# The second layer's experts in 64 slots each: plain float32 products on halves of the array's columns, weights unsplit, outputs summed to the tokens in PSUM

## The chip, the cores and the metric

The kernel runs on one core of a Trainium2 chip. The metric is the device time of one execution in microseconds (us); lower is better. The number compared is the median of several runs, three for the kernel before.

## The reference

A backbone of two layers works on 512 tokens of 1024 channels: 256 context tokens and 256 latent ones. Each layer has four token mixers side by side, an output projection, and then a mixture of 16 experts. The last layer's experts work on the 256 latent tokens alone, since only these are returned. A router chooses for each token the best of four groups of four experts and the two best experts in it. What an expert computes, in float32:

```python
def _moe(h, router_w, router_b, w_gate, w_up, w_down):
    scores = jax.nn.sigmoid(h.astype(F32) @ router_w.astype(F32))
    sel = scores + router_b.astype(F32)
    grp_score = lax.top_k(sel.reshape(-1, N_GROUPS, EXPERTS_PER_GROUP), TOP_K)[0].sum(-1)
    best = jnp.argmax(grp_score, axis=-1)
    in_grp = (jnp.arange(N_EXPERTS) // EXPERTS_PER_GROUP)[None, :] == best[:, None]
    _, idx = lax.top_k(jnp.where(in_grp, sel, -jnp.inf), TOP_K)
    w = jnp.take_along_axis(scores, idx, axis=-1)
    w = w / jnp.sum(w, axis=-1, keepdims=True)
    combine = jnp.sum(jax.nn.one_hot(idx, N_EXPERTS, dtype=F32) * w[..., None], axis=1)
    out = jnp.zeros(h.shape, F32)
    for e in range(N_EXPERTS):
        act = jax.nn.silu(h @ w_gate[e]) * (h @ w_up[e])
        out = out + combine[:, e:e + 1] * (act @ w_down[e])
    return out.astype(h.dtype)
```

Every expert has three matrices, 1024 x 512 (gate), 1024 x 512 (up) and 512 x 1024 (down): 6 MB, and 96 MB for the 16 experts of a layer. Each token needs two experts only, so a kernel can hand each expert just its own tokens. By the reference's routing the fullest expert of the second layer gets 61 of the 256 tokens.

## The kernel before, in words

Tokens are kept transposed (channels on the 128 partitions, tokens along the free axis, `xT`), in eight blocks of 128 channels. The program is written in the order of the model; a scheduler then puts the instructions of each engine into an order, by classes that the code sets with `k.order` and by the order of the code within a class. The change sits in the last stage of the second layer, `moe` (L1696), after which only the final norm and the output follow.

An expert's tokens. `route` (L1600) ranks each token within its two experts. `moe` turns the 256 latent tokens into rows and splits them in two parts, `h2_hi` and `h2_lo`, so that passes in the rounded format F32R carry float32 values exactly. `gather` (L1750) takes two experts at a time: a selection matrix `sel` of zeros and ones is multiplied with the rows (L1762, 32 passes, for each of eight blocks two parts by two tiles of tokens), and the outcome, the tokens of both experts transposed, goes to the tiles `xe` (L1766). An expert has `CAPS[1]` = 96 slots for its tokens. Where an expert had more tokens than slots, a branch (L1801) sends all tokens through every expert; it isn't taken on these inputs.

An expert's weights. They come as six loads of 1 MB, [128, 2048] each (`load`, L1937): two halves of gate (0, 1), two of up (2, 3), two of down (4, 5; these halve the output channels). The ring that they land in has two tracks of three buffers each, and load i goes to track i % 2:

```python
RINGS = (3, 3)
...
lambda e, i: load(I["w_moe"][16 * layer + e, i], which=i % 2)
```

All loads are issued by SP in one fixed order; a load waits there until the last reader of its buffer is done, and the loads behind it wait with it. The first six are asked for ahead of the branch. `parts` (L152, L153) splits each load into a high and a low tile of 1024 columns by two: two ScalarE (ACT) copies and two VectorE (DVE) subtractions per load. After these four the ring buffer is free.

An expert's products. Tokens are the stationary operand (96 columns of the array), weights the moving one, 512 columns at a time. `product` makes three F32R passes for each input block, 24 for gate, 24 for up and 24 for down:

```python
for i, ((xh, xl), (wh, wl)) in enumerate(zip(xs, ws)):
    nc.tensor.matmul(p, xh, wh, start=first and i == 0, stop=False)
    nc.tensor.matmul(p, xh, wl, start=False, stop=False)
    nc.tensor.matmul(p, xl, wh, start=False, stop=last and i == n - 1)
```

Between up and down stand the silu (L1849), the product with up (L1850), four transposes (L1856), and the split of the transposed activations (L1858, L1859). The code issues the next expert's gate product before this expert's down product.

Back to the tokens. The down products are copied out as rows `y` (L1877) and, for the first `VIA` = 15 experts, written to the DRAM tensor `Y` (L1881). Behind the 15th expert, GpSimd (POOL) fetches for each token its two rows from `Y` by indirect DMAs (L1891: `ya`, `yb`), and ACT and DVE weight and add them (L1893, L1894). The last expert's rows come back by a product with a weighted selection matrix, `backT` (L1901); `ya` is added to it in PSUM by products with the identity (L1905). Eight DVE additions put the sum, times the gate of the conditioning, onto `xT` (L1912). Then come the norm's sums of squares (L1319 to L1329), the scaling (L2022) and the output.

PSUM has eight banks: four of track a, two of b, two of p; the pools of 4 KB tiles (`TILES`) hold all that is called `u` in the code.

Of the kernel before, what the change touches and what calls it, by code (L numbers as in the profile page):

```python
# [19 lines left out]
# arguments of a sigmoid are kept above this: exp(-FLOOR) < 2^64, and the sigmoid there is 2e-19  # L20
# [3 lines left out]
def shape_consts():  # L24
    """Constants that depend on shapes alone, one [128, n] block per name."""
# [8 lines left out]
    # diagonal 32x32 blocks: [partition s, column r % 32]  # L34
# [42 lines left out]
# constants that the first steps take; the others follow later  # L77
# [3 lines left out]
class Consts:  # L81
    def __init__(self, nc, pool, src):
        """src: DRAM AP [128, n], the early ones first"""
# [28 lines left out]
class K:  # L112
    """What all parts of the kernel share: engines, pools, constants. Tiles come from the pools of the track (a or b):
    slots of a pool go out in program order, so that what runs side by side takes them from different pools."""
# [41 lines left out]
    def exp_ln(self):  # L156
        """Exp and Ln from one table of ScalarE, from here on"""
# [6 lines left out]
def sigmoid(nc, t):  # L164
    """t = 1 / (1 + t), t holding exp(-x), below 2^64 (what Ln takes)"""
# [11 lines left out]
    # log decays, rows: [token, tile, (dir h dk)], 16 times too large  # L177
# [13 lines left out]
    # cumulative sums within tiles of 128, transposed: [(h dk), token]  # L191
# [8 lines left out]
    # chunk states  # L200
# [30 lines left out]
    # scores within tiles, transposed: [s, h, tile, r]  # L231
# [24 lines left out]
    # two heads at a time, a bank for each  # L256
# [45 lines left out]
    # outputs, transposed  # L302
# [21 lines left out]
def norm_gate(k, oT, gT, center=False):  # L324
    """norm(oT) * silu(gT) in two parts, norms over groups of 64 partitions; all [128, 2, n]; gT is at least FLOOR"""
# [22 lines left out]
def ret(k, qT, kT, v, dlog, t0):  # L348
    """qT: [128 (h%2 dk), 2, tokens from t0*128 on], kT: [128, 2, 512], v: [128, 4, 256] rows,
    dlog: [128, 12] decay logits: (dir h) on all partitions, then (dir hp) by partition."""  # L350
# [9 lines left out]
    # decays  # L360
# [17 lines left out]
    # rotary embedding of the latent tokens  # L378
# [10 lines left out]
    # states  # L389
# [31 lines left out]
    # scores within tiles, transposed  # L421
# [41 lines left out]
def tri_inverse(nc, N, G, X, P):  # L463
    """G = inverse of (I + N), N strictly lower, one 32x32 matrix per partition at [col * 32 + row].
    G holds the identity at first. X: [128, 512] and P: four [128, 1024], scratch."""
# [5 lines left out]
    # pairs  # L471
# [14 lines left out]
    # 16: zero quarters of the triangles are skipped; columns split over the engines  # L486
# [3 lines left out]
    def dot(eng, out, left, right, nr, ncol, nk, scratch):  # L490
        """out[c, r] = sum_k left[k, r] * right[c, k]"""
# [20 lines left out]
def dn(k, dram, xs, cw, gab, prm, t0):  # L512
    """In five steps (a generator), the first four as soon as the projections of k, of the gates, of v and of q are there;
    the last yields the outputs. xs: calls for the q, k, v projections [128 (h%2 d), 2, tokens] (q: from t0*128 on);
    cw: [128, 6, 5] taps, gab: [128, 4, 16] rows (a: dir h | b: dir h), prm: [128, 16] (dt_bias | a_log),
    dram: two scratch tensors [128, 1024] f32."""
# [4 lines left out]
    def conv(n):  # L521
        """Short convolution, silu, unit norm of q and k"""
# [35 lines left out]
    def in_rows(y):  # L558
        """[token, tile, (h d)]"""
# [20 lines left out]
    # log decay and log beta, [token, tile, (dir h)]  # L580
# [14 lines left out]
    # decays from the chunk's start (times beta), to its end: chunks of 32, and of 64 (with the neighbour's sum)  # L595
# [23 lines left out]
    # the same of the later chunk of a pair (from its start) and of the earlier one (to its end): forward the odd ones  # L619
    # are later, backward the even ones  # L620
# [6 lines left out]
    # pair decays [s, dir, tile, h, r] in chunks of 32  # L627
# [19 lines left out]
    def products(y, dec, a):  # L647
        """Products of keys with y, by their decays; tiles from a on"""
# [21 lines left out]
    # inverses, one system (chunk, dir, tile, h) per partition  # L670
# [8 lines left out]
    # the blocks of these systems that link the chunks of a pair: [later token, tile, h, earlier]  # L679
# [38 lines left out]
    # [d][half of the systems] matrices 128 x 128, zeros but for the diagonal 32x32 blocks  # L718
# [15 lines left out]
    # the inverses of pairs of chunks: B, [column, system, row], gets minus later inverse @ link @ earlier inverse  # L734
# [961 lines left out]
def moe(k, I, P, S, h2, xT, mod, load_e, between, layer):  # L1696
# [53 lines left out]
    def gather(e):  # L1750
# [20 lines left out]
        for g in range(2):  # L1771
            if e + g < VIA:
                continue
# [284 lines left out]
```

## Time and profile before

| | |
|---|---|
| device time, median of 3 runs | 1637.6 us (1631.38 to 1642.4) |
| span of the profiled execution, first to last instruction | 1629.0 us |
| TensorE (PE) busy, of that span | 1457.5 us, 11752 instructions |
| VectorE (DVE) | 1164.8 us |
| ScalarE (ACT) | 841.8 us |
| GpSimd (POOL) | 379.7 us |
| mean granted clock of TensorE | 0.936 of full speed |
| bytes moved by DMA | 345.71 MB, mean 212 GB/s |

The profile is one execution on the chip, recorded by the hardware; its engines' busy times are sums over the whole program, in which the stages have different limits. The program has some 1300 us ahead of the second layer's experts, some 310 us of these experts, and some 20 us behind them, so the table alone says little about the stage that changes. The profiled execution's own time is given only as its span; the median of the runs is 8.6 us above it. In the profile's rows, PE stands for matmuls, PEld for the loading of their stationary operand, SPq for SP's queue of DMAs; "128*96 128x512" is a stationary operand of 128 rows and 96 columns with 512 moving columns on 128 partitions. A matmul of F32R is one instruction in the trace; one of plain float32 is two.

### The profile page before, as it was taken

To read this page: it belongs to the slowest core of one execution; us is meant where nothing else is said; L and a number is where in the kernel's file an instruction comes from. 1 tells how busy PE (TensorE), PEld (TensorE's weight loads), DVE (VectorE), ACT (ScalarE), POOL (GpSimd) and SP (SyncE) were. 2 spreads that over 40 slices of the span, in tenths; PEclk is the share of its full clock that TensorE was granted. 3 is DMA by queue.
4 is the path that set the end of the run, shared out by engine and by line. 5 is a ranking of instruction groups with operands and counts; after the bars stand their busy time and mean duration, and the time that the engine had idled before them with its cause. 6 is when DMAs were issued, how large, how long until landed. Compare 5 with 4: busy or idle time off the path is not lost. (4 is left out here: it accounts for less than half of the span.)

```text
span 1629.0 us, 29159 instructions
## 1 busy us (share of the span) xinstructions
PE 1457.5 (89%) x11752; PEld 1159.6 (71%) x11752; DVE 1164.8 (72%) x1696; ACT 841.8 (52%) x1192; POOL 379.7 (23%) x429
## 2 busy tenths in 40 slices
PE   5797879999997999999998788969999799999996
PEld 1686669888665788888886576758867577777774
DVE  6795792667435879787885786874467488888885
ACT  4442214342523758576773533313254488888874
POOL 2745242444210000000004665442242000000001
PEclk9897869999998999999999897969899799999999
DMA  9130352142445878889798221534366199999992
GB/s 387 48 111 27 98 176 103 66 149 100 143 159 203 322 285 348 323 306 363 276 349 320 70 78 57 171 126 140 122 238 239 37 356 351 347 337 362 356 336 103
DMA packets 85991, 345.71 MB, mean 212 GB/s; under 512 B 32582, under 2 KB 37512, under 8 KB 51160
## 3 DMA queue, kind: packets, MB, share of 16 engines
q1 hardware_dynamic: 79784, 320.36, 53.5%
q10 hardware_dynamic: 3840, 13.76, 2.1%
q0 software_dynamic: 2224, 9.63, 1.5%
q8 instruction: 96, 1.57, 0.4%
q14 instruction: 47, 0.39, 0.1%
HBM read 315.05 MB, written 28.67 MB: 211 GB/s over the span
## 5 line engine op out<-in xcount | busy, mean ns | idle before, releaser
L153 DVE TENSOR_TENSOR w_lo<-ring,w_hi 128x1024 fp32r<-128x1024 f32 x384 | 453.8, 1219 | 77.8 <-ACT w_hi L152 75.4
L152 ACT ACTIVATE w_hi<-ring 128x1024 fp32r<-128x1024 f32 x384 | 395.6, 1059 | 91.5 <-PE ps_up L1747 61.5
L1747 PE MATMUL ps_up<-w_lo,xe 128*128 128x512 f32 (+1 forms) x512 | 202.2, 395 | 4.9 <-DVE w_lo L153 4.4
L1746 PE MATMUL ps_up<-w_hi,xe 128*128 128x512 f32 (+1 forms) x512 | 200.5, 394 | 3.2 <-PEq L1801 3.2
L1748 PE MATMUL ps_up<-w_hi,xe 128*128 128x512 f32 (+1 forms) x512 | 200.7, 392 | 0.0
L1380 PE MATMUL ps_project<-h_hi,wi_lo 128*128 128x256 f32 (+1 forms) x568 | 138.9, 311 | 24.7 <-DVE wi_lo L153 24.6
L1380 PE MATMUL ps_project<-h_hi,wi_hi 128*128 128x256 f32 (+1 forms) x568 | 137.6, 310 | 14.3 <-ACT h_hi L1368 8.3
L1380 PE MATMUL ps_project<-h_lo,wi_hi 128*128 128x256 f32 (+1 forms) x568 | 135.0, 303 | 5.4 <-DVE h_lo L1369 5.4
L1380 PEld LDWEIGHTS ps_project<-h_hi,wi_lo 128*128 128x128 f32 (+1 forms) x568 | 99.0, 205 | 33.1 <-DVE wi_lo L153 28.0
L1747 PEld LDWEIGHTS ps_up<-w_lo,xe 128*128 128x128 f32 (+1 forms) x512 | 89.4, 175 | 33.8 <-DVE w_lo L153 9.7
L1380 PEld LDWEIGHTS ps_project<-h_hi,wi_hi 128*128 128x128 f32 (+1 forms) x568 | 98.9, 205 | 19.3 <-ACT h_hi L1368 8.4
L1746 PEld LDWEIGHTS ps_up<-w_hi,xe 128*128 128x128 f32 (+1 forms) x512 | 89.5, 175 | 28.9 <-ACT xe L1766 2.0
L1748 PEld LDWEIGHTS ps_up<-w_hi,xe 128*128 128x128 f32 (+1 forms) x512 | 89.5, 175 | 26.4
L1746 PE MATMUL ps_down<-w_hi,actT 128*128 128x512 f32 (+1 forms) x256 | 100.7, 395 | 5.7 <-ACT actT L1858 5.7
L1380 PEld LDWEIGHTS ps_project<-h_lo,wi_hi 128*128 128x128 f32 (+1 forms) x568 | 98.2, 203 | 8.9 <-DVE h_lo L1369 6.1
L1747 PE MATMUL ps_down<-w_lo,actT 128*128 128x512 f32 (+1 forms) x256 | 100.5, 393 | 1.2 <-DVE w_lo L153 1.2
L1748 PE MATMUL ps_down<-w_hi,actT 128*128 128x512 f32 (+1 forms) x256 | 96.9, 395 | 0.9 <-DVE actT L1859 0.4
L152 ACT ACTIVATE wi_hi<-ring 128x1024 fp32r<-128x1024 f32 (+1 forms) x50 | 51.2, 1032 | 88.1 <-DMA ring<-in_w_in 43.6
L1937 POOL DMA_DIRECT2D ring<-in_w_in x4 | 2.5, 618 | 385.0 <-DMA ring<-in_w_ada 374.8
L153 DVE TENSOR_TENSOR wi_lo<-ring,wi_hi 128x1024 fp32r<-128x1024 f32 (+1 forms) x50 | 69.8, 1401 | 25.3 <-ACT wi_hi L152 19.7
L1766 ACT ACTIVATE xe<-ps_gather 128x384 fp32r<-128x384 f32 (+1 forms) x96 | 48.0, 527 | 65.3 <-PE ps_gather L1762 65.3
L1891 POOL DMA_INDIRECT ya<-Y,rt_slot x6 | 5.8, 965 | 322.7 <-DVE w_lo L153 320.4
(534 smaller groups left out, 3159.7 us busy)
## 6 DMA issues: line engine op xcount, KB each, us to landing
ring<-in_w_moe SPq DMA_DIRECT2D x192, 1024.0 KB
ring<-in_w_ada SPq DMA_DIRECT2D x46, 1024.0 KB
ring<-in_w_in SPq DMA_DIRECT2D x21, 1024.0 KB
ring<-in_w_out SPq DMA_DIRECT2D x8, 1024.0 KB
Y<-y ACTq DMA_DIRECT2D x15, 512.0 KB
Y<-y ACTq DMA_DIRECT2D x15, 384.0 KB
xT<-in_xT SPq DMA_DIRECT2D x8, 512.0 KB
ring<-in_w_in POOLq DMA_DIRECT2D x3, 1024.0 KB
```

The source lines that it names most:

```text
L152: self.nc.scalar.activation(out[0], src, AF.Copy)
L153: self.nc.vector.tensor_tensor(out[1], src, out[0].bitcast(F32), ALU.subtract)
L1380: nc.tensor.matmul(p[:, c], x[a], w[b][:, c], start=i + a + b + o == 0, stop=i == n - 1 and a == 1, skip_group_check=True)
L1746: nc.tensor.matmul(p, xh, wh, start=first and i == 0, stop=False)
L1747: nc.tensor.matmul(p, xh, wl, start=False, stop=False)
L1748: nc.tensor.matmul(p, xl, wh, start=False, stop=last and i == n - 1)
L1766: nc.scalar.activation(x, p, AF.Copy)
L1891: nc.gpsimd.indirect_dma_start(out=o, out_offset=None, in_=Y[:VIA * cap], in_offset=bass.IndirectOffsetOnAxis(ap=slot[:, i, t:t + 1], axis=0))
L1937: queue.dma_start(w[:, :n], src)
```

## The change

The first layer keeps `moe`; two pieces of it become functions of their own, `token_rows` (the rows in two parts) and `overflow` (the branch), with the same code in them. The second layer gets a function of its own, `moe_small`:

- 64 slots per expert and not 96.
- `gather` takes four experts at a time, 256 columns in all, and sums the products of both parts of the rows in PSUM, so that `xe` is one float32 tile and not two parts.
- The weights are not split: the ring's buffers are read by the products themselves, in plain float32. An inward product uses 64 columns of the array; for each input block two matmuls of 256 moving columns, on the left and the right half of the array's columns, take the two halves of gate's (then up's) 512 outputs, which thus lie on the two halves of one PSUM bank's partitions.
- The silu and the product with up work on 128 partitions by 256 columns; two transposes bring the activations back.
- Outward, the two loads (halves of the output channels) go to the two halves of the array's columns, 512 moving columns each.
- Each expert's output is at once multiplied with its weighted selection matrix (`back`), in matmuls that use one half of the array's rows each, and summed over all 16 experts in four PSUM banks (`last`). There are no rows in DRAM and no indirect fetches.

```diff
-CAPS = (128, 96)
+CAPS = (128, 64)
...
+def token_rows(k, h2, nt):
...
+def overflow(k, I, h2, xT, mod, cwo, mxi, nt, cap, layer):
...
+def moe_small(k, I, P, S, h2, xT, mod, load_e, layer):
+    nc, C = k.nc, k.C
+    cap, nt = 64, 2
+    assert CAPS[layer] == cap
+    NT = nt * 128
+    q0 = T - NT
+    k.track = "b"
+    rsel, _, _, cwo, mxi, cw = route(k, h2, P, nt, cap)
+    hi, lo = token_rows(k, h2, nt)
+    def gather(e):
+        sel = k.u("sel", nt * 4 * cap).bitcast(F32R).rearrange("p (t g s) -> p t g s", t=nt, g=4)
+        nc.vector.tensor_tensor(sel, C["row_f"][:, None, None, :cap].to_broadcast([128, nt, 4, cap]),
+                                rsel[:, :, e:e + 4, None].to_broadcast([128, nt, 4, cap]), ALU.is_equal)
+        xs = [k.u("xe", track="b") for _ in range(2)]
+        out = [[] for _ in range(4)]
+        for m in range(0, 8, 2):
+            p = k.bank("gather", "b")
+            for i in range(2):
+                n = 0
+                for rows in (hi, lo):
+                    for t in range(nt):
+                        nc.tensor.matmul(p[:, i * 256:(i + 1) * 256], rows[t][:, (m + i) * 128:(m + i + 1) * 128],
+                                         sel[:, t].rearrange("p g s -> p (g s)"), start=n == 0, stop=n == 2 * nt - 1)
+                        n += 1
+            x = xs[m // 4][:, m % 4 * 256:(m % 4 + 2) * 256]
+            if m % 4:
+                nc.scalar.activation(x, p, AF.Copy)
+            else:
+                nc.vector.tensor_copy(x, p)
+            for i in range(2):
+                for g in range(4):
+                    out[g].append(x[:, i * 256 + g * cap:i * 256 + (g + 1) * cap])
+        return out, sel
+    def back(sel, e):
+        s = k.u("back", nt * 128).rearrange("p (t a s) -> p t a s", t=nt, a=2)
+        nc.vector.tensor_tensor(s, sel[:, :, e % 4].bitcast(F32)[:, :, None].to_broadcast([128, nt, 2, cap]),
+                                cw[:, :, e:e + 1, None].to_broadcast([128, nt, 2, cap]), ALU.mult)
+        p = k.bank("back", "b")
+        for t in range(nt):
+            nc.tensor.transpose(p[:, t * 128:(t + 1) * 128], s[:, t].rearrange("p a s -> p (a s)"), C["ident"])
+        b = k.u("backT", NT)
+        nc.vector.tensor_copy(b, p[:, :NT])
+        return b
+    xs, sel = gather(0)
+    first = [load_e(0, i) for i in range(6)]
+    overflow(k, I, h2, xT, mod, cwo, mxi, nt, cap, layer)
+    ps = [k.bank("last", "a") for _ in range(4)]
+    ps = [ps[m // 2][:, m % 2 * NT:(m % 2 + 1) * NT] for m in range(8)]
+    def inward(x, e):
+        p = k.bank("up", "p")
+        for j in (0, 2):
+            for half in range(2):
+                w = weight(e, j + half)
+                for i in range(4):
+                    for c in range(2):
+                        nc.tensor.matmul(p[64 * c:64 * c + 64, 128 * j:128 * j + 256], x[4 * half + i],
+                                         w[:, 512 * i + 256 * c:512 * i + 256 * c + 256], start=half + i == 0,
+                                         stop=half * 4 + i == 7, skip_group_check=True)
+        return p
+    def weight(e, i):
+        return load_e(e, i) if e else first[i]
+    after, asel = None, None
+    pu = inward(xs[0], 0)
+    for e in range(16):
+        act = k.u("act", 256)
+        nc.scalar.activation(act, pu[:, :256], AF.Silu)
+        nc.vector.tensor_tensor(act, act, pu[:, 256:], ALU.mult)
+        b = back(sel, e)
+        if e % 4 == 1 and e < 12:
+            after, asel = gather(e + 3)
+        p = k.bank("actT", "b")
+        for f in range(2):
+            nc.tensor.transpose(p[:, f * 128:(f + 1) * 128], act[:, f * 128:(f + 1) * 128], C["ident"])
+        aT = k.u("actT", 256)
+        nc.scalar.activation(aT, p[:, :256], AF.Copy)
+        ds = [weight(e, 4 + half) for half in range(2)]
+        if e < 15:
+            pu = inward((xs if e % 4 < 3 else after)[(e + 1) % 4], e + 1)
+        p = k.bank("down", "b")
+        for i in range(4):
+            c, f = divmod(i, 2)
+            for half in range(2):
+                nc.tensor.matmul(p[64 * half:64 * half + 64], aT[:, f * 128 + 64 * c:f * 128 + 64 * c + 64],
+                                 ds[half][:, 512 * i:512 * i + 512], start=i == 0, stop=i == 3)
+        y = k.u("y", 512)
+        nc.vector.tensor_copy(y, p)
+        for m in range(4):
+            for half in range(2):
+                hs = slice(64 * half, 64 * half + 64)
+                nc.tensor.matmul(ps[4 * half + m], y[hs, m * 128:(m + 1) * 128], b[hs], start=e + m % 2 == 0, stop=e == 15,
+                                 skip_group_check=True)
+        if e % 4 == 3:
+            xs, sel = after, asel
+    k.exp_ln()
+    for m, p in enumerate(ps):
+        x = xT(m, q0, T)
+        nc.vector.scalar_tensor_tensor(x, p, mod[:, 40 + m, 0:1], x, op0=ALU.mult, op1=ALU.add)
...
-            moe(k, I, P, S, h2, xT, mod[layer], lambda e, i: load(I["w_moe"][16 * layer + e, i], which=i % 2),
-                between, layer)
+            load_e = lambda e, i: load(I["w_moe"][16 * layer + e, i], which=i % 2)
+            if layer:
+                moe_small(k, I, P, S, h2, xT, mod[layer], load_e, layer)
+            else:
+                moe(k, I, P, S, h2, xT, mod[layer], load_e, between, layer)
```

The instructions ahead of the second layer's experts stand in the same order on every engine, and SP has the same 96 loads of the experts' weights in the same order. From the experts on the order differs. Below are rows of PE's order, the names as in the code (`consts_75` is the tile with the identity; "64x256 x8" are eight matmuls of 256 moving columns onto 64 partitions, and one load of inward weights has eight).

The first place is the first expert, on PE. Before, from its transposes on:

```order
L1856 MATMUL ps_actT<-consts_75,act 128x96 x4
L1747 MATMUL ps_up<-w_lo,xe 96x512
L1748 MATMUL ps_up<-w_hi,xe 96x512
L1746 MATMUL ps_up<-w_hi,xe 96x512
L1747 MATMUL ps_up<-w_lo,xe 96x512
L1748 MATMUL ps_up<-w_hi,xe 96x512
L1746 MATMUL ps_down<-w_hi,actT 96x512
L1747 MATMUL ps_down<-w_lo,actT 96x512
```

Now, from its `back` matrix and its transposes on:

```order
L1977 MATMUL ps_back<-consts_75,back 128x128 x2
L2015 MATMUL ps_actT<-consts_75,act 128x128 x2
L1996 MATMUL ps_up<-ring,xe 64x256 x8
L2026 MATMUL ps_down<-ring,actT 64x512 x8
L1996 MATMUL ps_up<-ring,xe 64x256 x16
L2033 MATMUL ps_last<-backT,y 128x256 x8
L1977 MATMUL ps_back<-consts_75,back 128x128 x2
L1996 MATMUL ps_up<-ring,xe 64x256 x8
```

Before, the transposes stand among the passes of one block of up; now they are followed by one load of the second expert's inward product (eight matmuls), the first expert's outward product (L2026), two more loads inward, and the sum over the tokens (L2033).

The second place is on PE behind the gather of experts 4 to 7 (L1957), which stands in expert 1 (counted from 0) behind the first eight matmuls of expert 2:

```order
L1957 MATMUL ps_gather<-sel,h_hi 128x256 x2
L1957 MATMUL ps_gather<-sel,h_lo 128x256 x2
L1996 MATMUL ps_up<-ring,xe 64x256 x8
L2015 MATMUL ps_actT<-consts_75,act 128x128 x2
L1996 MATMUL ps_up<-ring,xe 64x256 x8
L2026 MATMUL ps_down<-ring,actT 64x512 x8
L2033 MATMUL ps_last<-backT,y 128x256 x8
L1996 MATMUL ps_up<-ring,xe 64x256 x8
L1977 MATMUL ps_back<-consts_75,back 128x128 x2
```

Expert 1's transposes (L2015) stand behind the gather and the second load of expert 2's inward product, its outward product behind the third. Before, a gather for two experts stood behind the silu of every second expert.

The third place is the end of the experts, on PE. Before:

```order
L1748 MATMUL ps_down<-w_hi,actT 96x512
L1901 MATMUL ps_last<-backT,y 128x256 x9
L1905 MATMUL ps_last<-consts_75,ya 128x128 x3
L1901 MATMUL ps_last<-backT,y 128x256 x8
L1905 MATMUL ps_last<-consts_75,ya 128x128 x3
L1901 MATMUL ps_last<-backT,y 128x256 x7
L1905 MATMUL ps_last<-consts_75,ya 128x128 x10
L1322 MATMUL ps_rstd<-sq,consts_75 32x256 x8
```

Now:

```order
L1996 MATMUL ps_up<-ring,xe 64x256 x24
L1977 MATMUL ps_back<-consts_75,back 128x128 x2
L2015 MATMUL ps_actT<-consts_75,act 128x128 x2
L2026 MATMUL ps_down<-ring,actT 64x512 x8
L2033 MATMUL ps_last<-backT,y 128x256 x8
L1322 MATMUL ps_rstd<-sq,consts_75 32x256 x8
```

The products with the identity that added the fetched rows are gone; the last expert's inward product, transposes, outward product and sum now follow one another with nothing else among them.

## Rows read from the trace of the kernel before

**Rows 1.** Busy us of each engine (xinstructions), granted clock, DMA share, GB/s, by stretch.
```profile
core 0: us, PE busy (x) PEld busy (x) DVE busy (x) ACT busy (x) POOL busy (x), PEclk, DMA share, GB/s
1285.00:1292.00 7.00, 0.41 (x4) 0.32 (x4) 5.87 (x28) 0.95 (x3) 0.00 (x0) 0.67 0.00 0
1294.00:1302.00 8.00, 6.99 (x32) 6.82 (x32) 4.60 (x29) 5.19 (x9) 0.00 (x0) 0.56 0.01 4
1302.00:1610.00 308.00, 300.19 (x1446) 216.37 (x1446) 248.43 (x235) 247.57 (x315) 6.28 (x4) 1.00 0.89 333
```

**Rows 2.** What SP's queue waited for, 1303 to 1585: us, times, longest.
```profile
SPq L1937 <- DVE w_lo L153: 251.0, 90, 7.7
```

**Rows 3.** Groups of 1302 to 1610: busy us, mean ns of one | idle before.
```profile
L153 DVE TENSOR_TENSOR w_lo<-ring,w_hi 128x1024 fp32r<-128x1024 f32 x192 | 227.4, 1220 | 53.0 <-ACT w_hi L152 52.5
L152 ACT ACTIVATE w_hi<-ring 128x1024 fp32r<-128x1024 f32 x191 | 196.4, 1058 | 37.6 <-PE ps_up L1747 31.8 <-PE ps_down L1747 3.6 <-DVE w_lo L153 0.9
L1747 PE MATMUL ps_up<-w_lo,xe 128*96 128x512 f32 x256 | 100.7, 393 | 0.0
...
L1850 DVE TENSOR_TENSOR act<-act,ps_up 96x512 f32<-96x512 f32 x16 | 10.9, 680 | 2.7 <-PE ps_up L1748 2.2
L1849 ACT ACTIVATE act<-ps_up 96x512 f32<-96x512 f32 x16 | 9.3, 584 | 0.0
...
L1858 ACT ACTIVATE actT<-ps_actT 128x384 fp32r<-128x384 f32 x16 | 7.9, 491 | 8.3 <-PE ps_actT L1856 8.3
```

**Rows 4.** The chain that ended last: start us, us, what.
```profile
1601.45 3.38 POOL yb L1891
...
1605.13 5.35 DMA ya<-Y,rt_slot
...
1614.93 1.35 PE ps_last L1905 x12
1616.31 0.93 DVE xT L1912 x3
...
1617.49 0.88 DVE xT L1912 x2
```

**Rows 5.** PE in time: start us, us, instructions; matmuls on parts of the array.
```profile
1120.16 1.26 PE L779 MATMUL ps_dn<-dn_bd,dn_ke 128*64 128x128 f32 x20
...
1219.50 1.93 PE L1301 MATMUL ps_mods<-ring,sc 128*32 128x512 f32 x16
...
1229.63 1.16 PE L434 MATMUL ps_ret<-k_rq,k_rk 64*128 64x128 f32 x14
```

**Rows 6.** PE in time, 1254 to 1256: passes of 256 columns on the whole array.
```profile
1255.30 0.28 PE L1380 MATMUL ps_out_project<-mix_hi,wo_hi 128*128 128x256 f32 x1
1255.41 0.28 PE L1380 MATMUL ps_out_project<-mix_lo,wo_hi 128*128 128x256 f32 x1
```

**Rows 7.** PE in time, 1240 to 1242: column halves, then the whole array.
```profile
1240.16 0.44 PE L315 MATMUL ps_gla<-gla_A,k_gv 128*64 128x128 f32 x4
1240.53 0.71 PE L318 MATMUL ps_gla<-gla_qi,gla_s 128*128 128x128 f32 x4
```

**Rows 8.** Stretches at the program's start, columns as in rows 1.
```profile
10.00:20.00 10.00, 7.81 (x30) 1.74 (x30) 9.54 (x73) 5.54 (x9) 0.17 (x3) 1.00 1.01 419
20.00:30.00 10.00, 5.71 (x40) 2.92 (x44) 7.18 (x8) 0.99 (x2) 5.83 (x4) 0.90 1.02 414
30.00:40.00 10.00, 5.67 (x44) 2.55 (x36) 4.10 (x10) 3.31 (x7) 2.15 (x1) 0.84 1.02 421
```

**Rows 9.** SP's queue in time, 1304 to 1309: first new loads of the experts' stage.
```profile
1304.10 3.17 SPq L1937 DMA_DIRECT2D ring<-in_w_moe  x2
```

**Rows 10.** The us behind that first load, columns as in rows 1.
```profile
1304.00:1305.00 1.00, 1.00 (x6) 0.71 (x5) 0.51 (x2) 1.00 (x2) 0.00 (x0) 1.00 0.00 0
1305.00:1306.00 1.00, 1.00 (x5) 0.49 (x4) 1.00 (x2) 1.00 (x2) 0.00 (x0) 1.00 1.18 147
1306.00:1307.00 1.00, 1.00 (x5) 0.73 (x5) 1.00 (x2) 1.00 (x2) 0.00 (x0) 1.00 0.82 344
```

More of the change, by code (lines that the diff above doesn't have):

```diff
@@ L1693, in route @@
     return rsel, slot, wm, cwo, mxi, cw
-def moe(k, I, P, S, h2, xT, mod, load_e, between, layer):
+def token_rows(k, h2, nt):
     nc, C = k.nc, k.C
-    cap = CAPS[layer]
-    nt = 4 - 2 * layer
-    q0 = T - nt * 128
-    k.track = "b"
-    rsel, slot, wm, cwo, mxi, cw = route(k, h2, P, nt, cap)
     hi, lo = [], []
@@ L1716, in moe @@
             nc.vector.tensor_tensor(lo[t][:, c], p, a[:, c], ALU.subtract)
+    return hi, lo
+def overflow(k, I, h2, xT, mod, cwo, mxi, nt, cap, layer):
+    nc, C = k.nc, k.C
+    q0 = T - nt * 128
     def add(acc, t):
@@ L1731, in add, with chunk @@
                                                op1=ALU.add)
+    n = nc.values_load(mxi[:1], min_val=0, max_val=T)
+    with k.tc.If(n > cap):
+        NT = nt * 128
+        acc = [k.u("ov_acc") for _ in range(nt)]
+        wt = [k.u("ov_w", track="w") for _ in range(2)]
+        for a in acc:
+            nc.gpsimd.memset(a, 0.0)
+        with k.tc.For_i(0, 16, 1) as e:
+            def chunk(i):
+                return I["w_moe"][bass.ds(e + 16 * layer, 1), i].rearrange("a p (j n) -> p (a j) n", j=4)
+            act = []
+            for f in range(4):
+                ps = []
+                for i in (0, 2):
+                    w = wt[i // 2].rearrange("p (j n) -> p j n", j=8)
+                    for h in range(2):
+                        nc.sync.dma_start(w[:, 4 * h:4 * h + 4], chunk(i + h)[:, :, f * 128:f * 128 + 128])
+                    ps.append(k.bank("moe")[:, :NT])
+                    for j in range(8):
+                        nc.tensor.matmul(ps[-1], w[:, j], h2(j), start=j == 0, stop=j == 7)
+                if f % 2 == 0:
+                    act.append(k.u("ov_act"))
+                a = act[-1][:, (f % 2) * NT:(f % 2 + 1) * NT]
+                nc.scalar.activation(a, ps[0], AF.Silu)
+                nc.vector.tensor_tensor(a, a, ps[1], ALU.mult)
+            for half in range(2):
+                c = slice(512 * half, 512 * half + 512)
+                for h in range(2):
+                    w = wt[h].rearrange("p (j n) -> p j n", j=2)
+                    nc.sync.dma_start(w, chunk(4 + half)[:, 2 * h:2 * h + 2])
+                    for t in range(nt):
+                        p = k.bank("moe")
+                        for f in range(2):
+                            o = f * NT + t * 128
+                            nc.tensor.matmul(p, act[h][:, o:o + 128], w[:, f], start=f == 0, stop=f == 1)
+                        nc.vector.scalar_tensor_tensor(acc[t][:, c], p, cwo[:, t, 0:1], acc[t][:, c], op0=ALU.mult,
+                                                       op1=ALU.add)
+            tmp = k.u("ov_tmp", 64).rearrange("p (t e) -> p t e", t=4)[:, :nt]
+            nc.vector.tensor_copy(tmp[:, :, :15], cwo[:, :, 1:])
+            nc.vector.tensor_copy(cwo[:, :, :15], tmp[:, :, :15])
+        for t in range(nt):
+            add(acc[t], t)
@@ L1733, in split_into, with moe @@
+def moe(k, I, P, S, h2, xT, mod, load_e, between, layer):
+    nc, C = k.nc, k.C
+    cap = CAPS[layer]
+    nt = 4 - 2 * layer
+    q0 = T - nt * 128
+    k.track = "b"
+    rsel, slot, wm, cwo, mxi, cw = route(k, h2, P, nt, cap)
+    hi, lo = token_rows(k, h2, nt)
     def split_into(hi, lo, src):
```

51 lines of the change are left out of this document (9 added, 42 removed).

## The prediction

> **What bounds the kernel now.** I read the busy times by stretch first [rows 1]. The second layer's sixteen experts run from 1302 to 1610 us: 308 us, 19.25 us per expert. The reader is to see three things there: TensorE (PE) is busy 300 of 308 us at the full clock, VectorE and ScalarE 248 us each, and the transfers have a share of 0.89 at 333 GB/s. Three resources are close together, so next I asked who waits for whom on SP's queue [rows 2]: all 90 loads of weights waited for the lower halves of an earlier load, 251 us in total. The ring is full all the time; a load is asked for when a buffer comes back, so the transfers follow the compute and not the other way round. The groups of that stretch [rows 3] say what gives the buffers back late: each 1 MB load is split by two ACT and two DVE instructions of 1.06 and 1.22 us (12.7 us of ACT and 14.6 us of DVE per expert), and PE does three passes of 512 columns per input block, 72 per expert. Last comes the chain at the end [rows 4]: at 1601 it leaves PE for the fetch of the earlier experts' rows from DRAM (POOL 3.38 us, DMA 5.35 us); the last matmul of the sum ends at 1616.3 us, 12.7 us before the span's end at 1629.0.
>
> So PE binds, and anything that shortens it meets the transfers next.
>
> **The change part by part.** Only the second layer's experts change; on every engine the instructions before them stand in the same order.
>
> *Products.* A plain float32 matmul counts as two instructions in the trace. On column halves, 20 instructions of 128 moving columns take 1.26 us [rows 5]; less the 0.16 us by which each lasts longer than its turn, that is ten pairs of 0.11 us. Two halves, each with moving columns of its own, thus run side by side. The quarters of L1301 give the same price with 512 columns: 16 instructions in 1.93 us, four at a time, 0.43 us. An expert's inward products are 32 matmuls of 256 columns: 32 pairs of instructions at 0.216 us, 6.9 us. The outward ones are 8 matmuls of 512: 8 pairs at 0.43 us, 3.45 us.
>
> *Sum in PSUM.* 8 matmuls of 256 columns on halves of the rows. L434 has 14 such instructions of 128 columns in 1.16 us [rows 5], too little for one after another (14 × 0.107 = 1.5), so pairs: 8 × 0.216 = 1.73 us. One after another it would be 3.45; I take the pair and keep the other for the range.
>
> *Gather and transposes.* 32 passes of 256 columns per four experts at 0.12 us [rows 6]: 0.96 us per expert. Four transposes at 0.11: 0.44.
>
> *Switches of the array's shape*, about six per expert. Four instructions of L315 on column halves begin at 1240.16 and last 0.44; less the 0.16 us of tail their columns end at 1240.44, and L318 on the whole array begins at 1240.53 [rows 7]: 0.09 us each, 0.5 per expert. The Trainium skill, "TensorEngine Tiling (Array Packing)", Key Properties, says that a change of tiling mode drains TensorE, which speaks against mixing three shapes in one expert; this trace agrees, with 0.09 us. If the switch were free, the time below would be some 2 us less, since PE would mostly wait longer for loads instead.
>
> PE's work is thus 6.9 + 3.45 + 1.73 + 0.96 + 0.44 + 0.5 = 14.0 us per expert. To this comes the chain silu, product, transpose, copy: 0.58 + 0.68 + 0.49 us for 512 columns [rows 3], about 0.4 each for 256. Where no other matmul stands in between it costs some 1.5 us; in the order it mostly costs 0.6. So PE needs 14.6 us per expert, against 19.25.
>
> *Splits and rows through DRAM* go: 196 us of ACT and 227 of DVE, 15 writes of Y, the two fetches. Beside PE's 300 us they were cover, so they are worth nothing themselves, but for the 10 us chain at the end. What is late there next is the last outward product.
>
> *Loads.* 96 as before. With several asked for ahead the queue moved 414 to 421 GB/s at a share of 1.0 [rows 8]; 1.049 MB at 421 GB/s is 2.49 us per load, 15.0 us per expert. A load asked for with the queue empty starts late: asked at 1304.10 [rows 9], it has moved nothing by 1305 and only 0.49 MB by 1307 [rows 10]; I reckon 4.9 us to landing, 2.4 more than in a row.
>
> PE's 14.6 and the queue's 15.0 us are nearly equal, and six buffers hold one expert only, so the sum is not the larger of the two. I laid PE's new order beside SP's fixed order of loads at these prices. An example, from the second place of the order in the section on the change: expert 1's outward product stands behind three of expert 2's inward loads and the gather. It ends near 1342, and until then its two loads hold two of six buffers. SP cannot ask for expert 2's outward halves before, nor for anything behind them. What was asked for earlier has landed by 1337.6; the next load comes at 1350 and not at 1340: 10 us lost. There are such gaps of 1 to 10 us behind the first two experts and behind each of the three gathers, in all some 37 us. In the order's last third the queue streams.
>
> At full clock: first load asked for at 1304, 4.9 to land, 89 × 2.49 = 222, gaps 37: the last lands at 1568. Behind it stand the outward product 3.45, copy 0.8, sum 1.7: 1574. PE waits for loads 42 us in this lay-out, up to 7 us at once. In [rows 1] the clock fell to its lower level (1.2 GHz) around the 7 us without matmuls and its mean was 0.56 for the next 8 us. In the lay-out some 50 us of the stage would run at 1.2 GHz, with half of that covered by waits: 12 us, 1586. For what I laid out too smoothly I add 2: the last matmul at 1588 instead of 1616.3, 28 us less.
>
> *Behind it* nothing changes but that eight additions of 0.3 to 0.4 us (three and two of them stand with 0.93 and 0.88 us in [rows 4]) follow the last product together and not three ahead: 13.2 us instead of 12.7, so the gain stays about 28. The span goes from 1629.0 to 1601. That execution's span is 8.6 us below the runs' median of 1637.6; with the same 8.6 around it I predict 1610 us (1.7% less).
>
> **Rivals.**
> 1. *The queue streams without gaps.* For it: loads and PE need 15.0 and 14.6 us. Against: the order of buffers above. 1304 + 4.9 + 222 + 6 = 1537 for the last matmul, 1559 us. It would take slack that I don't see. Chance 0.08.
> 2. *No change: loads cost what they cost in this stage.* 333 GB/s at share 0.89 [rows 1] is 374 GB/s of busy queue, 2.80 us per load and not 2.49. For it: it is the same data in the same place. Against: there the queue ran dry again and again, and each restart is part of that share; [rows 8] had no restarts. The lay-out then gives 1607 for the last matmul, 1629 us. If in addition the sum ran one row half after another, some 5 us more. Chance 0.21.
> 3. *Slower: the low clock holds.* PE now has waits in each expert, where before it had almost none. At 1.2 GHz its 14.0 us of work become 28 per expert. For it: the 0.56 of [rows 1]. Against: in 20 to 40 us PE was busy only 57% of the time and still had 0.84 to 0.90 [rows 8]; a slow engine stops waiting, which brings the clock back. Each us of work at 1.2 GHz costs half a us; from about 56 us of it beyond my 50, a third of the stage, the gain is gone. With half of the stage's 290 us so, 145/2 − 12 = 60 us more: 1670 us. Chance 0.07.
> 4. *The halves don't run side by side when they accumulate.* Then the products cost 20.7 us and not 10.35, 25 us per expert and 400 in all: the last matmul at 1716, 1738 us. [Rows 5] speak against it; it decides as soon as a pair of 256 columns costs over 0.35 us. Chance 0.04.
>
> That the branch for tokens beyond 64 slots runs is out: by the reference's routing of its own inputs the fullest expert of the second layer gets 61.
>
> **How the numbers follow.** My forecast has 0.60; its own range, from full clock (1574, 1596 us) to unpaired sum and more waits, is 1592 to 1627. Over 1% (16 us) is about what a measurement of this kernel can tell from no change. Faster by that: 0.56 of the forecast's 0.60, rival 1, and 0.06 of rival 2: 0.70. Within 1%: 0.04 and 0.12 of rival 2: 0.16. Slower: 0.03 of rival 2 and rivals 3 and 4: 0.14. A range of 1583 to 1645 leaves out rivals 1, 3 and 4, 0.19.
>
> **What would show it.** Right: L1996 in pairs of 0.216 us; SP's waits no longer on L153 but on the outward product (L2026); PE waiting for ring loads some 40 us, longest early; last matmul near 1588; DVE and ACT below 60 us each in the stage. Wrong: pairs at 0.43 (rival 4), a granted clock under 0.8 over the stage (3), landings 2.8 us apart in a full queue (2), or no waits on loads at all (1).

## The result and the profile after

| | before | changed |
|---|---|---|
| device time, median | 1636.4 us (4 runs, 1631.4 to 1642.4) | 1574.9 us (4 runs, 1568.7 to 1584.0) |
| ratio | | 0.9627, 95% interval 0.9583 to 0.9672 |
| span of the profiled execution | 1629.0 us | 1574.6 us |
| stage: first gather matmul to last matmul of the sum | 322.8 us (from 1294.4) | 253.8 us (from 1307.3) |
| behind the stage | 11.9 us | 13.5 us |

It is faster by 3.7%, more than twice the 1.7% forecast, and below the range's lower end of 1583 us. The stage is 69 us shorter. The two spans differ by 54 only: the changed kernel's profiled execution reached the stage 12.9 us later, although every instruction ahead of it is the same, and what stands behind the stage took 1.6 us longer. The part ahead of the stage varies with the clock: for instance 1130 to 1150 us had 0.77 before and now was wholly at the lower level (0.50). So from here on kernels are compared by the stage. (A stage is measured to the end of the last matmul's record; the chain, which the first expectations used, lets it end 0.8 us earlier: 253.0.)

The stretches of the stage before, then of the changed kernel's, columns as in [rows 1]:

```profile
1294.40:1316.00 21.60, 20.29 (x89) 15.78 (x90) 15.77 (x37) 18.58 (x24) 0.00 (x0) 0.85 0.49 171
1316.00:1617.20 301.20, 293.39 (x1443) 213.52 (x1441) 241.07 (x233) 238.10 (x305) 6.28 (x4) 1.00 0.88 329
```

```profile
1307.30:1329.00 21.70, 19.44 (x143) 13.91 (x145) 5.69 (x31) 3.25 (x5) 0.00 (x0) 0.93 0.53 199
1329.00:1561.10 232.10, 216.77 (x1588) 124.07 (x1584) 35.58 (x73) 16.25 (x37) 0.00 (x0) 1.00 0.96 389
```

PE's work is what went: it was busy 313.7 us of the stage before and is busy 236.2 us now, 77.5 less, where the stage is 69 shorter. It is still busy most of the time, now beside transfers at 389 GB/s and a share of 0.96 (0.89 at 333 in [rows 1]). DVE and ACT have 41 and 20 us of work left. The clock is full for all 232 us: of the 50 us at the lower level that the prediction laid out there is nothing but the start. What PE waited for (us, times, longest), from 1285 us on:

```profile
PE ps_route L1659 <- DVE rt L1657: 6.6, 1, 6.6
PE ps_up L1996 <- DMA ring<-in_w_moe: 5.2, 4, 1.9
PE ps_down L2026 <- ACT actT L2017: 4.5, 9, 0.5
```

The first is the router, ahead of the stage. On loads PE waited 5.2 us where 42 were laid out. And what SP's queue waited for, which answers to [rows 2]:

```profile
SPq L2064 <- PE ps_up L1996: 93.9, 50, 5.8
SPq L2064 <- PE ps_down L2026: 62.6, 15, 6.3
```

Of these 65 waits of SP for buffers only 15 are for an outward product, none over 6.3 us (ten more, 26 us together, end at other products of PE). The chain that ended last, at the last two experts (start, us, what):

```profile
1540.02 3.65 PE ps_down L2026 x16
...
1547.33 5.35 PE ps_up L1996 x48
...
1554.56 3.79 PE ps_down L2026 x16
...
1559.12 1.18 PE ps_last L2033 x8
1560.30 0.93 DVE xT L2040 x3
```

24 inward matmuls are 48 instructions in 5.35 us, 0.223 us for each pair of instructions; 8 outward ones, 16 instructions, take 3.65, 0.456 a pair. The POOL and DMA pieces of [rows 4] are gone. The last load landed at 1554.64, when the last outward product, which needs it, had just begun (1554.56): loads and PE come out even there.

### The profile page after: what moved, and what is told of

Read it like the earlier page. It is cut to its first block, busy times and chain, and to the rows that moved or that the text cites. A ratio compares the mean times of both kernels' runs of the same rounds, so it can differ in the third digit from the quotient of the medians.

```text
span 1574.6 us, 28837 instructions
## 1 busy us (share of the span) xinstructions
PE 1390.1 (88%) x11950; PEld 1077.8 (68%) x11950; DVE 949.7 (60%) x1534; ACT 605.4 (38%) x908; POOL 372.1 (24%) x425
## 5 line engine op out<-in xcount | busy, mean ns | idle before, releaser
L153 DVE TENSOR_TENSOR w_lo<-ring,w_hi 128x1024 fp32r<-128x1024 f32 x192 | 226.4, 1219 | 24.6 <-ACT w_hi L152 22.7
L152 ACT ACTIVATE w_hi<-ring 128x1024 fp32r<-128x1024 f32 x192 | 198.3, 1059 | 53.5 <-PE ps_up L1805 31.7
L1996 PE MATMUL ps_up<-ring,xe 128*64 128x256 f32 x1024 | 120.8, 382 | 7.4 <-DMA ring<-in_w_moe 5.2
L1996 PEld LDWEIGHTS ps_up<-ring,xe 128*64 128x64 f32 x1024 | 72.0, 137 | 53.1 <-issue 14.9
L1805 PE MATMUL ps_up<-w_lo,xe 128*128 128x512 f32 x256 | 101.6, 397 | 4.9 <-DVE w_lo L153 4.3
L1804 PE MATMUL ps_up<-w_hi,xe 128*128 128x512 f32 x256 | 100.2, 394 | 1.9 <-PEq L1735 1.9
L1806 PE MATMUL ps_up<-w_hi,xe 128*128 128x512 f32 x256 | 100.0, 391 | 0.0
L2029 DVE COPY y<-ps_down 128x512 f32<-128x512 f32 x16 | 11.1, 692 | 88.4 <-PE ps_down L2026 88.4
L2026 PE MATMUL ps_down<-ring,actT 128*64 128x512 f32 x256 | 58.6, 596 | 4.5 <-ACT actT L2017 4.5
L1805 PEld LDWEIGHTS ps_up<-w_lo,xe 128*128 128x128 f32 x256 | 48.1, 188 | 17.7 <-DVE w_lo L153 9.0
L1804 PEld LDWEIGHTS ps_up<-w_hi,xe 128*128 128x128 f32 x256 | 48.1, 188 | 12.0 <-ACT xe L1824 2.1
L1806 PEld LDWEIGHTS ps_up<-w_hi,xe 128*128 128x128 f32 x256 | 48.1, 188 | 9.1
```

The source lines that it names most:

```text
L152: self.nc.scalar.activation(out[0], src, AF.Copy)
L153: self.nc.vector.tensor_tensor(out[1], src, out[0].bitcast(F32), ALU.subtract)
L1996: nc.tensor.matmul(p[64 * c:64 * c + 64, 128 * j:128 * j + 256], x[4 * half + i], w[:, 512 * i + 256 * c:512 * i + 256 * c + 256], start=h ...
L2026: nc.tensor.matmul(p[64 * half:64 * half + 64], aT[:, f * 128 + 64 * c:f * 128 + 64 * c + 64], ds[half][:, 512 * i:512 * i + 512], start=i ...
L2029: nc.vector.tensor_copy(y, p)
```

## The experiments

The theory came from the built program. The loads' gaps in the prediction's lay-out (37 us) rest on each load taking the buffer of the load six before it, but the built program has other buffers: within a track of three, the ring's pool hands out the buffer that comes free first. Read from the program's addresses (buffers A to F; expert.load):

```
0.0 C  0.1 E  0.2 B  0.3 F  0.4 A  0.5 D
1.0 C  1.1 E  1.2 B  1.3 F  1.4 C  1.5 E
2.0 A  2.1 D  2.2 B  2.3 F  2.4 A  2.5 D
```

Expert 1's outward halves (1.4, 1.5) don't wait for expert 0's outward product (A, D); they follow into C and E as soon as expert 1's own first two inward loads are used. Expert 2's outward halves (2.4, 2.5), the prediction's example, take the buffers of 2.0 and 2.1 and don't wait for expert 1's outward product. The rival: PE's own work fills the stage whatever the buffers do.

A median is of 2 to 10 runs (e12: one), and its ratio is to runs of the kernel before on the same chip; the last column is PE's wait on loads in the profile, in us.

| run | median us | ratio to before | stage starts | stage us | waits |
|---|---|---|---|---|---|
| changed kernel | 1574.9 | 0.963 | 1307.3 | 253.8 | 5.2 |
| e1 six behind | 1621.6 | 0.989 (0.984 to 0.994) | 1305.2 | 300.5 | 32.9 |
| e2 six behind, half loads | 1581.2 | 0.964 | 1310.2 | 255.4 | 4.7 |
| e3 gather, high part alone | 1564.1 | 0.954 | 1299.9 | 253.8 | 4.6 |
| e4 before, 64 slots | 1645.5 | 1.002 (0.999 to 1.005) | 1301.6 | 329.9 | 0 |
| e5 changed kernel again | 1568.5 | 0.960 (0.955 to 0.966) | 1299.5 | 252.4 | 3.0 |
| e6 four loads ahead | 1578.0 | 0.963 (0.959 to 0.967) | 1305.4 | 266.7 | 14.7 |
| e7 the same, gather high | 1573.4 | 0.960 (0.956 to 0.964) | 1308.3 | 252.1 | 9.6 |
| e8 halves in blocks | 1602.5 | 0.979 | 1295.7 | 289.4 | 0.2 |
| e9 more buffers | 1566.8 | 0.955 (0.951 to 0.959) | 1305.0 | 254.6 | 4.4 |
| e10 more buffers, gather high | 1565.9 | 0.956 (0.952 to 0.960) | 1298.6 | 252.4 | 4.8 |
| e11 six behind, order free | 1577.3 | 0.962 | 1296.4 | 263.8 | 2.4 |
| e12 e10 once more | 1573.5 | 0.960 | 1305.4 | 253.1 | 6.5 |

**e1: the lay-out, built.** The stage's matmuls and transposes are written out in the changed kernel's own PE order and pinned to it; only the buffers and SP's order differ, and the order by no more than three swaps of neighbouring loads, all behind load 4.0 and so behind the place shown below:

```diff
-        return load_e(e, i) if e else first[i]
+        while issued[0] < 6 * e + i:
+            issued[0] += 1
+            a, b = divmod(issued[0], 6)
+            pin(nc.sync.dma_start(first[b], I["w_moe"][16 * layer + a, b]))
+        return first[i]
```

> The changed kernel with its own order on PE written down, but each load of weights goes to the buffer of the load six before it, in the order expert by expert, as the prediction's lay-out had it. Stage means from the first matmul of the first gather to the end of the last matmul of the sum: 253.0 us in the changed kernel (322 before). Theory A (the gaps of the lay-out are right for such buffers, the changed kernel has others): stage 285 to 300 us, 35 us longer from waits on loads alone, up to 47 if the clock falls in these waits; PE waits 30 to 40 us for loads; time near 1615. Theory B (PE's own work fills the stage whatever the buffers do, the lay-out's restarts are too dear): stage 253 to 260 us, time near 1580.

Measured: 300.5 us, 46.7 more, PE waiting 32.9 us for loads. Theory A, at the upper end of its stage.

```profile
PE ps_up L2009 <- DMA ring<-in_w_moe: 32.6, 8, 7.0
```

The whole stage of e1, three stretches of it, and then the same three of the changed kernel:

```profile
1305.20:1605.80 300.60, 255.38 (x1728) 148.63 (x1728) 41.39 (x104) 19.53 (x42) 0.00 (x0) 0.94 0.78 315
...
1340.00:1350.00 10.00, 9.34 (x63) 6.54 (x64) 1.23 (x2) 0.60 (x1) 0.00 (x0) 0.83 0.74 308
1350.00:1360.00 10.00, 9.11 (x64) 4.73 (x64) 0.85 (x2) 0.98 (x2) 0.00 (x0) 1.00 0.10 18
1360.00:1370.00 10.00, 2.96 (x18) 1.63 (x16) 0.84 (x2) 0.38 (x1) 0.00 (x0) 0.73 1.01 424
```

```profile
1340.00:1350.00 10.00, 10.00 (x84) 7.43 (x84) 1.38 (x2) 1.58 (x3) 0.00 (x0) 1.00 0.98 383
1350.00:1360.00 10.00, 9.11 (x66) 4.63 (x63) 1.96 (x4) 0.39 (x1) 0.00 (x0) 1.00 0.98 392
1360.00:1370.00 10.00, 10.00 (x72) 5.51 (x70) 1.54 (x3) 0.77 (x2) 0.00 (x0) 1.00 0.99 361
```

In e1 the queue stands still while PE works towards expert 1's outward product (18 GB/s), then PE stands still while the queue fills up (2.96 of 10 us), and the clock falls to 0.73 there. This is the place that the prediction gave as its example, with 10 us lost: load 2.4 is asked for at 1357.97, behind expert 1's outward product, and the queue loses 12.3 us; in the changed kernel it is asked for at 1340.11, behind an inward product, 20 us earlier in the stage. SP's waits on the outward product show it as well (15 times, 62.6 us in the changed kernel):

```profile
SPq L1999 <- PE ps_down L2048: 164.5, 18, 22.3
```

**e2: are these waits for transfers?** Of each later load only `first[b][:, :1024]` is brought.

> As the run before, but of each of the 90 later loads only the first half of the columns is brought (0.5 MB); the rest of the buffer keeps older weights, so the output is not the reference's. Theory A (waits for transfers): PE's waits on loads fall to 7 to 10 us and the stage to 258 to 265 us. Theory B (buffers and transfers have no part): the stage stays within 3 us of the run before. If it is SP's order of buffers alone and not the transfer's length: within 10 us of the run before.

255.4 us and 4.7 us of waits: theory A, better than its numbers. So the 45 us between e1 and e2 come from transfers that begin late: 28 us are waits of PE for loads, and most of the rest goes with the lower clock (0.94 over e1's stage; e2 has 0.92 in its first 22 us and 0.99 behind them).

**e11: such buffers, another order.** The changed kernel's code with `nc.sync.dma_start(first[i], ...)` kept in program order, PE's order left to the scheduler.

> As the first run (each load into the buffer of the load six before it, expert by expert), but the scheduler is free to choose PE's order for that. It then puts each expert's outward product further forward. Theory A (the 47 us of the first run came from that order of PE with those buffers, not from such buffers as such): stage 260 to 268 us, some 10 us above the changed kernel. Rival (six buffers taken in turn cost 35 us or more in any order): 285 to 300 us.

263.8 us: theory A, with 2.4 us of waits on loads. The same six buffers in turn cost 47 us in the one order and some 10 in the other.

**e5: once more.**

> The changed kernel once more, on the chip and among the runs of the three that follow. Stage (first matmul of the first gather to the last of the sum) 253 to 254 us as in its first profile, since nothing in it depends on what ran before; where the stage starts differs by some us with the clock granted in the unchanged part (1294 to 1310 us in the six profiles so far). If the gain were a matter of one lucky execution, the stage would differ by over 5 us.

252.4 us, a start at 1299.5, 1568.5 us: 1.4 us below the first profile's 253.8, a little more than expected and far from 5.

**e3, e6, e7: what bounds now.** e3 sums only `rows in (hi,)` in `gather`; e6 asks for expert 1's four inward loads ahead of the router's end; e7 does both.

> The changed kernel with 64 of the 128 gather passes left out (the low part of the tokens' rows is not added, so the output is slightly off): 7.7 us less work for PE, the loads the same. Theory A (with the pool's buffers PE binds, transfers are hidden): stage 6 to 8 us shorter than the changed kernel's 253.0, 245 to 247. Rival (the stream of loads, 15.0 us per expert, binds as much as PE): under 3 us shorter, 250 to 253.

> The changed kernel, but the second expert's four inward loads go, as halves of 0.5 MB, into eight 4 KB tiles that this stage has free, and are asked for before the router's end: four loads (10.0 us of the stream) fewer behind the first release of a buffer. Theory A (the stream of loads and PE's work each need the whole stage; taking work from one alone gives little): stage 3 to 6 us shorter, 248 to 251, PE then binding. Rival 1 (the loads alone bind): 10 us shorter, 244. Rival 2 (PE alone binds): under 2 us.

> The run before, and of the gather only the high part of the tokens' rows (64 of 128 passes left out, so the output is slightly off). Theory A (both bind): together they give 9 to 12 us, stage 242 to 245, although the lesser gather alone gave nothing. Rival 1 (the loads alone bind): the same 10 us as four loads ahead alone would give, 244, and that run too. Rival 2 (PE alone binds, and the lesser gather gave nothing for some other reason): within 2 us of 253.8.

e3: 253.8, no gain: nearest to the rival. Its last load landed 6.9 us before the last matmul ended (6.5 in the changed kernel), less than half a us before the last outward product began, so its end doesn't tell loads from PE either; its first 21 us had a clock of 0.82 (0.93). e6 missed every expectation: 266.7 us. The scheduler had chosen another order for PE and the loads, and PE waited 14.7 us in 15 places. e7, again in another order, gave 252.1, rival 2's number. These three don't tell PE from the loads, since the order changed with them (in e3 too); so e9 and e10 hold PE's order fast.

**e9, e10, e12: more buffers, PE's order pinned.** Free 4 KB tiles, two to a load, take the inward loads of every second expert. The expectation speaks of eight tiles, four more buffers; the built program uses twelve, so there are six more:

```diff
+    def wide(e, i):
+        ts = [k.u("early", track="w") for _ in range(2)]
+        for a, t in enumerate(ts):
+            nc.sync.dma_start(t, I["w_moe"][16 * layer + e, i][:, 1024 * a:1024 * a + 1024])
+        return ts
...
+            got[6 * e + i] = wide(e, i) if e % 2 and i < 4 else load_e(e, i)
```

> The changed kernel with its own order on PE held fast, and four more buffers for weights: the inward loads of every second expert go as halves into eight 4 KB tiles that the stage has free, the second expert's before the router's end. The earlier run with four loads ahead let the scheduler choose another order on PE; this one doesn't. Theory A (stream and PE both need the stage; with more buffers PE alone binds): no waits of PE on loads, stage 248 to 251 us against 252.4 and 253.8. Rival 1 (the loads alone bind): 240 to 244. Rival 2 (halves of 0.5 MB or the other order of loads cost the queue more): above 254.

> The run before, and of the gather only the high part of the tokens' rows (64 of 128 passes left out, so the output is slightly off): 7.7 us less for PE. Theory A: with the loads ahead the lesser gather now counts in full, stage 6 to 8 us below the run before, 241 to 245, while alone it gave nothing. Rival 1 (the loads alone bind): within 2 us of the run before. Rival 2 (the lesser gather costs nothing on PE, its passes hide): within 2 us as well, with the same busy time of the gather's rows; the busy time tells the two apart.

> The kernel of the run e10 once more (ten buffers, high part of the gather alone). There PE had some 6 us less to do than in e9 and the stage was only 2.2 us shorter, while the clock showed 0.84 in the stage's first 21 us (0.91 in e9) and 0.83 in one stretch of 10 us later (1.00 in e9). If the lower clock was that execution's own: a clock of 0.91 or more at the start, no later dip, and a stage of 247 to 249 us. If the lesser work brings it about: again 0.81 to 0.85 at the start, a dip later, and 251 to 253 us.

e9: 254.6 us. That is the number of rival 2, but not its reason: the queue isn't late. A stretch near the end of e9:

```profile
1540.00:1550.00 10.00, 10.00 (x84) 5.91 (x82) 1.02 (x2) 0.00 (x0) 0.00 (x0) 1.00 0.01 2
```

The queue is done at 1540 us, PE works on until 1559.5, and the stage is no shorter. Less the 4.4 us of waits on loads, 250 us are left: PE's work needs nearly the whole stage by itself, and loads that come sooner win nothing. (In the changed kernel the loads have nothing to spare either, as its last landing shows.) Then e10's lesser gather should count. PE's time from each gather matmul to the next one, added up over the stage, fell from 19.2 us in e9 to 12.4; the stage fell by 2.2 only, and theory A missed. Two rows of e10, against 0.91 in e9's first 21 us and 1.00 in its second stretch:

```profile
1298.60:1320.00 21.40, 18.82 (x124) 12.68 (x126) 5.69 (x30) 3.25 (x5) 0.00 (x0) 0.84 0.52 191
...
1380.00:1390.00 10.00, 9.34 (x50) 4.64 (x52) 1.02 (x2) 0.00 (x0) 0.00 (x0) 0.83 1.01 417
```

(21.4 × 0.07) + (10 × 0.17) is 3.2 us lost to the lower clock, and the inward matmuls took longer by about that (124.1 us against 120.8). e12, the same kernel again, had 253.1 us, 0.88 in its first 22 us, 0.94 and 0.89 from 1380 to 1400, and 6.5 us of waits on loads (4.4 in e9): the dip came back, the low start only in part, and neither of its two expectations holds in full. So what the lesser gather gives is mostly taken back by the clock and by waits, in both executions. Whether the lesser work brings the lower clock about stays open. The four profiles with the lesser gather have 0.82 to 0.89 in their first 21 to 22 us; of the eight of the changed code with the whole gather six have 0.91 to 0.93, but e1 and e8 have 0.81 and 0.82.

**e8: do halves run side by side?** The loops over the column halves and over the four input blocks are exchanged:

```diff
-                for i in range(4):
-                    for c in range(2):
+                for c in range(2):
+                    for i in range(4):
```

> The changed kernel with the inward matmuls of each load in another order: four on the left half of the columns, then four on the right, and not by turns. Same matmuls, same loads, same sums. Theory A (neighbours on different halves run side by side, 0.22 us a pair; those on one half follow one another): of eight matmuls only the two at a change of sides overlap, 6 units of 0.22 us instead of 4, 0.44 us more per load, 64 loads: stage 28 us longer, up to 57 us if nothing overlaps (8 units of 0.22 instead of 4). Rival (a plain matmul on 64 columns costs 0.11 us by itself, and halves have no part in it): stage unchanged.

289.4 us, 35.6 more: theory A, between its two numbers. One load's eight inward matmuls (16 instructions) of e8, then of the changed kernel:

```profile
1407.29 2.86 PE L1996 MATMUL ps_up<-ring,xe 128*64 128x256 f32 x16
```

```profile
1342.10 1.95 PE L1996 MATMUL ps_up<-ring,xe 128*64 128x256 f32 x16
```

**e4: one part alone.** `CAPS = (128, 64)` in the kernel before.

> The kernel before with 64 slots instead of 96 in the second layer and nothing else: one part of the change alone. The passes with weights keep 512 moving columns, so only the gather shrinks: 224 passes of 128 columns instead of 192, 0.027 us each, 6 us of PE, and the transposes by 64 columns. Theory A (slots alone give next to nothing): stage 312 to 318 us instead of 322, time 0.2 to 0.6 per cent below before. Rival (fewer slots are a main part of the gain): over 1 per cent.

No gain (1.002, 0.999 to 1.005), the rival is out, and the expected 6 us are missing too. Two rows of e4's gather and two of the same gather before:

```profile
1340.94 0.39 PE L1762 MATMUL ps_gather<-sel,h_hi 128*128 128x128 f32 x2
1341.16 0.39 PE L1762 MATMUL ps_gather<-sel,h_lo 128*128 128x128 f32 x2
```

```profile
1370.98 0.39 PE L1762 MATMUL ps_gather<-sel,h_hi 128*128 128x192 f32 x2
1371.20 0.38 PE L1762 MATMUL ps_gather<-sel,h_lo 128*128 128x192 f32 x2
```

Each row is two passes, and the rows follow one another by 0.22 us with 128 columns as with 192: 0.11 us per pass. That the stage came out 7 us longer is mostly clock: 0.72 in its first 21 us (0.85 before) is 2.8 us, and 0.66 from 1620 to 1630, where the end of the stage before had 1.00, is 3.4.

## Why the prediction was wrong

The direction, the mechanism and the prices hold; the size of one term was wrong, and a second hung on it.

- *PE binds, and the change takes PE's work away*: right. Pairs at 0.223 us (0.216 forecast), outward pairs at 0.456 (0.43), the sum in pairs, 8 matmuls in 1.93 us (1.73), gather passes at 0.12. With these, 14.0 us of PE's work per expert become 14.6. From one expert to the next it took 14.5 us near the end (the sums begin at 1530.86 and 1545.40 in the chain), with the wait for the silu chain but without a gather; 253.8 us are 15.9 per expert. Pairing on column halves is a main part of the gain: without it in the inward products alone (e8), 35.6 of the 69 us are lost. No run takes the splits or the rows through DRAM away alone; that they were worth nothing themselves is argued from PE's busy time, not shown.
- *The price of a load in a full queue, 2.49 us, and of one in an empty queue, 4.9*: right; where the queue is full most landings follow one another by 2.48 to 2.50 us, and the first new load took 4.90.
- *"SP cannot ask for expert 2's outward halves before, nor for anything behind them ... in all some 37 us"*: this is the step that failed. The 90 later loads of the changed kernel took 239.6 us from the first request (1315.0) to the last landing (1554.6); less 4.9 and 222 that leaves 12.7 us of gaps, not 37. SP could ask for expert 2's outward halves earlier, since they got other buffers than the lay-out gave them. The cause is shown by e1: with the lay-out's buffers the gaps are there, and at the place foretold. Their size was not exact: 285.6 us from e1's first request to its last landing leave some 59 us of gaps, at a lower clock, where 37 were laid out and 14 added for clock and margin; PE waited 32.9 us (42 laid out).
- *The clock, 12 us, and 2 more for smoothness*: not there, and neither were the waits beside which the clock was to fall. In e1, where they were, it stood at 0.94 over the stage, and around the end of six of PE's eight waits for inward loads it was at its lower level. The prediction's stage, 1294.4 to 1588, was 293.6 us; the kernel that it describes is e1, with 300.5.
- The sum: 24.3 us of gaps, 14 of clock and margin, 2.0 because the first load was asked for 7.7 and not 9.7 us into the stage, and 0.3 behind the last load make 40.6 us, and 293.6 − 253.0 is 40.6.
- *Rival 1*, the queue without gaps, was the nearest, with a chance of 0.08. Its 1559 us would need the gaps to vanish altogether; "slack that I don't see" was the pool's choice of buffers, which could be read from the built program. *Rivals 3 and 4* didn't come true, and in rival 2 the loads' price was wrong (2.49, not 2.80).
- *Behind the stage*: 14.3 us from the end in the chain, by which the 13.2 were forecast (13.5 from the end of the matmul's record): 1.6 more than before and not 0.5. *The 8.6 us between span and median*: the thirteen other profiles reached the stage at 1295.7 to 1310.2 us, 1303.0 on the mean, that of before at 1294.4. So adding it was right: most of it was that execution's early start, and 1.7 to 2.1 us is what a run's time has above its span wherever both are on record. The changed kernel's profile started 12.9 us later with 0.3 between span and median; with the 1.1 behind the stage this makes the 40.6 us of the stage some 35 in the median.

## What to carry to other kernels

Where a queue of loads feeds on buffers that come back, the order of the readers and the assignment of the buffers decide together: the same six buffers and the same matmuls cost 0, 10 or 47 us here. So read from the built program which buffer each load gets and for which instruction it waits, before laying out the queue; a rotation assumed is a guess. And a term for the clock that is laid out on waits is no second, separate cost: with 33 us of waits the stage had 0.94 (e1), with 5 us it had full clock behind its start.

## What the runs showed of the hardware that was not expected

An F32R pass on the whole array came every 0.11 us with 128 moving columns and with 192 (e4), 0.12 with 256: fewer columns per pass gave nothing there, fewer passes do. And some 7 us less work for PE, in a stage of which PE's work takes 250 us of 254.6 (e9), shortened it by 2.2 and 1.5 us (e10 and e12), beside a lower granted clock in both.
